# A hybrid backbone's instruction order planned with other costs, its chunk products alternating between row halves, its dense pages moved by 32 bytes

## The chip, the cores and the metric

The kernel runs on one core of one Trainium2 chip. TensorE (PE, with its weight loads PEld), VectorE (DVE), ScalarE (ACT) and GpSimd (POOL) compute; SyncE (SP) issues nearly all DMAs. The metric is the device time of one execution in microseconds, as a median of runs. Lower is better.

## The reference

Two layers over 512 latent tokens and 256 context tokens of width 1024, all in float32. The first mixes by windowed attention and by a bidirectional RWKV-7 scan, the second by a two-dimensional Fourier transform per channel group; each is followed by a squared-ReLU MLP of width 4096. Norms are adaptive (shift, scale and gate come from the conditioning vectors). Cut to what matters:

```
z = h @ w_in ; zc = hc @ w_in                       # one input projection, both streams
att = window_attention(q, k, v, kc, vc, sink)       # softmax over a window, all context keys, a sink
S <- S diag(w) - (S kk)(kk*a)^T + v k^T ; y = S r   # RWKV-7, both directions, context state first
x = x + gt1 * (concat(att, rw) @ w_out)
x = x + gt2 * (square(relu(h2 @ w1)) @ w2)          # channel MLP, both layers
f = fft2(h groups, axes=(tokens, channels)).real @ fourier_w_out   # mixer of the second layer
out = rmsnorm(x, final_g)                           # latent stream only
```

The context stream is not needed after the first layer's mixer, so the kernel computes for it only what the scan's start state and the attention's context keys take.

## The kernel before

**Numbers.** Dense products are made in float32r: each operand is split into a high part (ACT, a cast) and a low part (DVE, a subtraction), and `mm3` issues three matmuls: low x high, high x high, high x low. A weight page is 128x512 (`st` by DMA, then `whi`, `wlo`); a moving page is 128x512 (`hhi`/`hlo` for the normalised stream, `zhi`/`zlo` for the MLP's hidden values). Small products (scan, inverses, attention's value product) are plain float32, which the chip runs as two passes, so each has two records in the profile.

**Stages.** Adaptive norm of layer 0 and the input projection (to about 200 us), the scan, the inverses and attention (to about 560 us), the output projection, MLP 0 (to about 960 us), the Fourier mixer (to about 1060 us), MLP 1.

**The scan.** It runs in chunks of 64 tokens, two directions at once. Six pairs of token blocks (i = 0 to 5; 0 and 1 are context) have two chunks each (j). For a pair, `prep` loads pages (th, kk, r, k) that were spilled to DRAM and makes per chunk and direction the tiles `pr` (key and receptance, scaled by the decay) and `gq`. `chunkmats` multiplies them (`ps<-pr,gq`): for each half `hh` of the partitions (two heads are stacked on 128 partitions) four products `hp`, one tile of PSUM per half, which DVE masks into `ab` and `ed`. `ed` goes to DRAM and comes back later. `inverse` inverts the triangular blocks of `ab` with DVE, small DMAs of 16 KB and 32x32 matmuls. `chain_u`, `chain_s`, `chain_y` are the serial scan over the chunks.

**The order.** `body` doesn't issue anything. It records every operation with the `Plan` class; line 657 then issues all of them, so nearly every instruction has that line in the profile. `Plan.solve` is a list scheduler: it gives every operation a rank (longest way to the end by the costs of `cost`), and simulates the five engines. Whenever an engine is free it takes the ready operation with the highest rank. On the way it models:

- TensorE's granted clock: windows of `WIN` = 3413.3 ns, an activity share above `WARM` switches to full clock, one under `COLD` back to half; `fill` puts `warm` matmuls (line 647) into gaps. A matmul with another tile shape than the last (`r.mode`) costs `MODE` = 100 ns more; among the eight best, one of the same shape is preferred if its key is within `STICK`.
- DMAs: a queue with one server `srv`; a transfer ends 750 ns after its service. SP issues in the order of the plan, and an issue that has to wait holds all behind it.
- Memory: a tile is claimed by the first operation that uses it. If no buffer is free, the operation is parked; when any tile is released, the parked ones are tried again in the order in which they were parked. PSUM's eight banks are shared by four kinds (`mm`, `rk`, `ch`, `iv`), and `BANKS` says how many of them each kind can count on: a claim has to leave those of the other kinds free.

**Memory places.** The pools `const`, `wp`, `H` come first; then `P0`, `P` and `Q` follow each other at one place. `Q`'s pages, tag `zq` (34 of them), hold the hidden values of the MLPs and the Fourier stage's tiles. Tiles start at multiples of 32 bytes. `body` declares a small tile ahead of Q's others, which nothing reads or writes:

```
    Q.tile([128, 8], F32, name="zpad")
```

`solve` keeps only tiles that are used, `self.tiles = {m: t for m, t in self.tiles.items() if t["uses"]}`, so zpad isn't placed before. In the compiled program before, the `zq` pages start at multiples of 64 bytes, the pages of `H` 32 bytes past a multiple of 64.

Of the kernel before, what the change touches and what calls it, by code (L numbers as in the profile page):

```python
# [5 lines left out]
F32 = mybir.dt.float32  # L6
# [197 lines left out]
class Rec:  # L204


    __slots__ = ("eng", "op", "args", "kw", "acc", "lead", "n", "claims", "mode", "load", "piece")
# [31 lines left out]
class Plan:  # L239
# [5 lines left out]
    WIN, COLD, WARM = 3413.3, 0.27, 0.66  # L245
    MODE, STICK = 100, 1500
    KEEP, RAISE, SPARE = 0.7, 0.9, 100
    RING = {"mm": 3, "rk": 2, "ch": 2, "iv": 1}
    BANKS = {"mm": 2, "rk": 1, "ch": 2, "iv": 1}
# [87 lines left out]
    def cost(self, r):  # L337
# [4 lines left out]
        if r.eng == "tensor":  # L342
# [3 lines left out]
            r.mode = up(k), up(m)  # L346
# [4 lines left out]
            f = {(128, 128): 1.0, (64, 128): 0.95, (128, 64): 0.58 if w <= 64 else 0.49 if w <= 128 else 0.27, (64, 64): 0.53, (128, 32): 0.12}.get(r.mode, 0.47)  # L351
# [3 lines left out]
            h = f * (w / 1.2 + 4) if w >= 64 else 110.0 * f if w < 16 else f * (w + 3)  # L355
            r.load *= min(1.0, w / 1.2 / h)
            return 2 * h, h + max(245, w / 1.2 + 175)
        if r.eng == "scalar":
            d = 185 + 0.86 * n
            if r.op == "activation" and any(isinstance(r.kw.get(x), bass.AP) for x in ("scale", "bias")):  # L360
                d += 70
            if abs(ins[0].ap[-1][0]) > 1:
                d += 0.85 * n
            return max(d - 96, 55), d
        if r.eng == "vector":
# [3 lines left out]
            if r.op == "tensor_scalar" and n > 64:  # L369
                d -= 0.3 * n  # L370
            return max(d - 83, 55), d
# [8 lines left out]
        return max(d - 45, 55), d  # L380


    def solve(self):
# [60 lines left out]
        srv, lastmode = 0.0, None  # L444
# [77 lines left out]
        while sched < n:  # L522
# [17 lines left out]
            if e == "tensor" and lastmode:  # L540
                c = []
                while avail[e] and len(c) < 8:
                    c.append(heapq.heappop(avail[e]))
                pick = 0
                for q, (x, kk) in enumerate(c):
                    if recs[kk].mode == lastmode and x < c[0][0] + self.STICK:
                        pick = q
                        break
                k = c.pop(pick)[1]
# [6 lines left out]
            if e == "tensor":  # L556
                if lastmode and r.mode != lastmode:
                    t += self.MODE
                lastmode = r.mode
                c = clock(t)  # L560
                busy(t, hold / c, r.load)
                hold, lat = hold / c, lat - hold + hold / c
            start[k], te[e], end[k] = t, t + hold, t + lat
            if r.op == "dma_start":
# [14 lines left out]
                end[k] = srv + 750  # L579
# [24 lines left out]
            if rel and parked:  # L604
                pq, parked[:] = parked[:], []
# [8 lines left out]
    def issue(self, tc):  # L614
# [12 lines left out]
        def pool_of(name):  # L627
            if name not in pools:
# [4 lines left out]
                place.append(name)  # L633
            return pools[name]
# [31 lines left out]
def body(tc, I, out):  # L666
# [497 lines left out]
    def chunkmats(i, j):  # L1164
# [6 lines left out]
        for d in range(2):  # L1171
# [3 lines left out]
            for hh in range(2):  # L1175
                rows = slice(64 * hh, 64 * hh + 64)
# [933 lines left out]
```

## Time and profile before

| | |
|---|---|
| median of 3 runs | 1420.98 us (1417.09 to 1421.83) |
| profiled execution: time, span | 1418.5 us, 1416.7 us |
| granted TensorE clock, mean | 0.962 |
| PE busy | 1339.2 us (95%), 10752 matmuls |
| PEld busy | 1088.7 us (77%) |
| DVE / ACT / POOL busy | 816.6 (58%) / 642.1 (45%) / 326.7 us (23%) |
| DMA moved | 204.69 MB, 144 GB/s |

Matmuls are pipelined: one of 512 columns lasts some 390 ns in the profile, but the next starts some 230 ns after it. So "busy" says little of how fast PE goes, and rates have to be read as a count in a stretch of time. Granted clock is 1.00 at full speed and 0.50 where the throttle halves it. "SPq" is SP's time to issue, "issue" time in which an engine waited for nothing that the profile shows. An idle engine that is not on the chain costs nothing.

### The profile page before, as it was taken

How to read it: one execution, taken by the hardware profiler on the slowest of the kernel's cores; microseconds unless marked ns; L12 is line 12 of the kernel's file. 1: busy time of each engine (PE TensorE's matmuls, PEld its weight loads, DVE VectorE, ACT ScalarE, POOL GpSimd, SP SyncE). 2: the span in 40 equal slices, each digit the busy share in tenths (PEclk: the TensorE clock that was granted, in tenths of full speed). 3: DMA queues.
4: the chain of work that ended last, by engine and by line, in shares of the span. 5: the costliest groups of instructions: out<-in, count | busy, mean ns of one | idle time of the engine just before them, and what ended most of it. 6: DMA issues, size and time to landing. Idle time of an engine off the chain costs nothing.

```text
span 1416.7 us, 27647 instructions
## 1 busy us (share of the span) xinstructions
PE 1339.2 (95%) x10752; PEld 1088.7 (77%) x10752; DVE 816.6 (58%) x1516; ACT 642.1 (45%) x1289; POOL 326.7 (23%) x359
## 2 busy tenths in 40 slices
PE   6999989979888999999999999999989999999997
PEld 2787877767757777878887888878977888888886
DVE  3844497776876344778655566675976332333334
ACT  3775576365452225446522345333636522255322
POOL 1546485344361413050000000000560000000001
PEclk9999998989987899999999999999999999999999
DMA  9468975565545213226655565662312322223222
GB/s 366 155 193 266 300 243 168 123 174 151 143 117 153 79 34 103 89 76 201 193 171 185 179 190 183 195 199 68 105 61 81 103 91 96 97 91 104 90 89 75
DMA packets 173939, 204.69 MB, mean 144 GB/s; under 512 B 52008, under 2 KB 87912, under 8 KB 173808
## 3 DMA queue, kind: packets, MB, share of 16 engines
q1 hardware_dynamic: 171920, 200.99, 45.5%
q8 instruction: 84, 1.38, 0.4%
q10 hardware_dynamic: 1376, 1.90, 0.4%
q14 instruction: 47, 0.39, 0.1%
q0 software_dynamic: 512, 0.03, 0.0%
HBM read 177.41 MB, written 25.43 MB: 143 GB/s over the span
## 4 chain that ended last, share of the span: by engine, by line
PE 75%; DVE 10%; DMA 5%; issue 3%; ACT 3%; SPq 2%; POOL 1%; DVEq 0%; ACTq 0%; POOLq 0%
PE ps L657 74%; SPq L657 2%; DMA st<-adaA_in 1%; DVE wlo L657 1%; DVE ht L657 1%; DVE gq L657 1%; DMA st<-adaB_in 1%; DMA st<-win_in 1%; DVE Minv L657 1%; DVE wb L657 0%; PE warm L647 0%; DVE ab L657 0%; POOL pgth L657 0%; DVE fwlo L657 0%; DMA st<-fw_in 0%
## 5 line engine op out<-in xcount | busy, mean ns | idle before, releaser
L657 ACT CAST whi<-st 128x512 fp32r<-128x512 f32 x306 | 187.6, 620 | 414.6 <-PE ps L657 376.6
L657 DVE TENSOR_TENSOR wlo<-st,whi 128x512 fp32r<-128x512 f32 x306 | 223.7, 741 | 220.2 <-ACT whi L657 161.7
L657 PE MATMUL ps<-hlo,whi 128*128 128x512 f32 x600 | 230.9, 396 | 2.8 <-DVE hlo L657 2.8
L657 PE MATMUL ps<-hhi,whi 128*128 128x512 f32 x600 | 230.6, 397 | 1.9 <-ACT hhi L657 1.7
L657 PE MATMUL ps<-hhi,wlo 128*128 128x512 f32 x600 | 228.2, 396 | 0.3 <-DVE wlo L657 0.3
L657 PE MATMUL ps<-zhi,whi 128*128 128x512 f32 (+1 forms) x528 | 203.2, 389 | 1.9 <-ACT whi L657 1.9
L657 PE MATMUL ps<-zlo,whi 128*128 128x512 f32 (+1 forms) x528 | 202.2, 389 | 0.0
L657 PE MATMUL ps<-zhi,wlo 128*128 128x512 f32 (+1 forms) x528 | 199.5, 390 | 1.0 <-DVE wlo L657 1.0
L657 PEld LDWEIGHTS ps<-hlo,whi 128*128 128x128 f32 x600 | 113.5, 190 | 27.0 <-DVE hlo L657 4.3
L657 PEld LDWEIGHTS ps<-hhi,whi 128*128 128x128 f32 x600 | 113.2, 189 | 27.2 <-ACT hhi L657 2.6
L657 PEld LDWEIGHTS ps<-hhi,wlo 128*128 128x128 f32 x600 | 113.4, 189 | 23.8 <-DVE wlo L657 0.8
L657 PEld LDWEIGHTS ps<-zhi,whi 128*128 128x128 f32 x528 | 98.8, 188 | 25.5 <-ACT whi L657 3.2
L657 PEld LDWEIGHTS ps<-zhi,wlo 128*128 128x128 f32 x528 | 98.8, 188 | 25.0 <-DVE wlo L657 2.8
L657 PEld LDWEIGHTS ps<-zlo,whi 128*128 128x128 f32 x528 | 98.7, 188 | 22.2
L657 POOL TENSOR_TENSOR rs<-ms,pw 128x4 f32<-128x4 f32 (+1 forms) x7 | 6.2, 886 | 408.1 <-DVE ms L657 408.1
L657 POOL TENSOR_TENSOR wa<-st 128x512 f32<-128x512 f32 x8 | 14.4, 1797 | 342.6 <-DMA st<-fw_in 322.1
L657 POOL TENSOR_TENSOR ada<-ada,sB 128x512 f32<-128x512 f32 x48 | 65.7, 1389 | 33.4 <-DMA ada<-adaB_in 24.9
L657 DVE CUSTOM_DVE_ANT_0 st<-st,sB,vec 128x512 f32<-128x512 f32 x56 | 43.0, 768 | 43.2 <-DMA st<-adaB_in 42.3
L657 DVE TENSOR_TENSOR zlo<-s,zhi 128x512 fp32r<-128x512 f32 x64 | 44.2, 691 | 27.0 <-ACT zhi L657 26.8
L657 PE MATMUL ps<-pr,gq 64*128 64x128 f32 (+1 forms) x384 | 43.5, 328 | 11.2 <-DVE gq L657 11.2
L657 PEld LDWEIGHTS ps<-pr,gq 64*128 64x128 f32 x384 | 39.1, 228 | 17.5 <-issue 9.2
L657 DVE CUSTOM_DVE_ANT_0 st<-st,sB,adv 128x512 f32<-128x512 f32 x56 | 41.9, 749 | 10.0 <-DMA st<-adaB_in 9.4
(401 smaller groups left out, 2557.1 us busy)
## 6 DMA issues: line engine op xcount, KB each, us to landing
st<-w_in SPq DMA_DIRECT2D x256, 256.0 KB, 2.7
st<-adaB_in SPq DMA_DIRECT2D x112, 256.0 KB, 3.2
ada<-adaB_in SPq DMA_DIRECT2D x48, 256.0 KB, 4.6
st<-win_in SPq DMA_DIRECT2D x40, 256.0 KB, 4.4
spl_th<-th SPq DMA_DIRECT2D x16, 384.0 KB, 4.8
pgth<-spl_th SPq DMA_DIRECT2D x24, 256.0 KB, 4.3
st<-adaA_in SPq DMA_DIRECT2D x16, 256.0 KB, 5.1
st<-adaA_in SPq DMA_DIRECT2D x8, 512.0 KB, 7.8
```

What stands on the lines that cost most here:

```text
L657: i = getattr(getattr(tc.nc, r.eng), r.op)(*[tr(a) for a in r.args], **{x: tr(a) for x, a in r.kw.items()})
```

## The change

**The planner's numbers.** `COLD` goes from 0.27 to 0.30 and `WARM` from 0.66 to 0.64. The cost of a float32 matmul is no longer a factor by tile shape: `full` is its time alone (bounded by the weight load), `side` how many run beside each other; `r.place` is the row and column place in the array that it uses (from the partitions of its operands), `taken` how long it holds that place. A matmul waits for its own place; one with another tile shape waits for all places plus `MODE` (`on_array`); among the best eight of one shape, the one whose place is free first is taken. An ACT instruction costs 95 ns for each of scale and bias that is a tensor (70 ns for either or both before); a scan on DVE costs 350 ns more; a DMA ends 1000 ns after its service, not 750; SP can't be more than `DEPTH` = 2400 ns ahead of the DMA server. Parked operations are tried by rank, not by age. `rk` can count on two banks of PSUM instead of one. All these alter the order only.

**chunkmats.** The two PSUM tiles are taken ahead of the products, and the products alternate between the halves: (hp 0, hh 0), (hp 0, hh 1), (hp 1, hh 0) and so on. The masks follow after all eight.

**zpad.** The tile is taken out of `body` and allocated in `issue`, when the pool Q is opened. Q's other tiles start 32 bytes later.

```diff
@@ -204,7 +204,7 @@
 class Rec:
 
 
-    __slots__ = ("eng", "op", "args", "kw", "acc", "lead", "n", "claims", "mode", "load", "piece")
+    __slots__ = ("eng", "op", "args", "kw", "acc", "lead", "n", "claims", "mode", "load", "piece", "place", "taken")
 
 
 class Queue:
@@ -242,11 +242,11 @@
 
     ENGS = ("tensor", "vector", "scalar", "gpsimd", "sync")
     WAIT = {"tensor": 54, "vector": 33, "scalar": 32, "gpsimd": 60, "sync": 60}
-    WIN, COLD, WARM = 3413.3, 0.27, 0.66
-    MODE, STICK = 100, 1500
+    WIN, COLD, WARM = 3413.3, 0.30, 0.64
+    MODE, STICK, DEPTH = 100, 1500, 2400
     KEEP, RAISE, SPARE = 0.7, 0.9, 100
     RING = {"mm": 3, "rk": 2, "ch": 2, "iv": 1}
-    BANKS = {"mm": 2, "rk": 1, "ch": 2, "iv": 1}
+    BANKS = {"mm": 2, "rk": 2, "ch": 2, "iv": 1}
 
     def __init__(self, nc):
         self.nc = nc
@@ -343,22 +343,25 @@
             lhs, rhs = r.args[1], r.args[2]
             k, m, w = lhs.ap[0][1], self.size(lhs), self.size(rhs)
             up = lambda v: 32 if v <= 32 else 64 if v <= 64 else 128
-            r.mode = up(k), up(m)
+            r.mode, r.place, r.taken = (up(k), up(m)), None, 0
             r.load = k * m / 16384
             if rhs.dtype == F32R:
                 r.load *= w / (w + 32.6)
                 return w / 2.4 + 13.6, w / 2.4 + 185
-            f = {(128, 128): 1.0, (64, 128): 0.95, (128, 64): 0.58 if w <= 64 else 0.49 if w <= 128 else 0.27, (64, 64): 0.53, (128, 32): 0.12}.get(r.mode, 0.47)
             if r.op == "transpose":
                 r.load *= 0.49
                 return 109.0, 281.0
-            h = f * (w / 1.2 + 4) if w >= 64 else 110.0 * f if w < 16 else f * (w + 3)
-            r.load *= min(1.0, w / 1.2 / h)
-            return 2 * h, h + max(245, w / 1.2 + 175)
+
+            full = max(w / 1.2 + 4, 111 if m > 64 else 50 if m > 32 else 14 if w < 32 else 27)
+            side = {(64, 128): 1.9, (128, 64): 1.85, (64, 64): 1.8, (128, 32): 4.0, (32, 32): 1.7}.get(r.mode, 1.0)
+            r.place = lhs.offset // lhs.ap[0][0] // r.mode[0], r.args[0].offset // r.args[0].ap[0][0] // r.mode[1]
+            r.taken = 2 * full
+            r.load *= min(1.0, w / 1.2 / full) * side
+            return 2 * full / side, full + max(245, w / 1.2 + 175)
         if r.eng == "scalar":
             d = 185 + 0.86 * n
-            if r.op == "activation" and any(isinstance(r.kw.get(x), bass.AP) for x in ("scale", "bias")):
-                d += 70
+            if r.op == "activation":
+                d += 95 * sum(isinstance(r.kw.get(x), bass.AP) for x in ("scale", "bias"))
             if abs(ins[0].ap[-1][0]) > 1:
                 d += 0.85 * n
             return max(d - 96, 55), d
@@ -368,6 +371,8 @@
                 d += 0.25 * n
             if r.op == "tensor_scalar" and n > 64:
                 d -= 0.3 * n
+            if r.op == "tensor_tensor_scan":
+                d += 350
             return max(d - 83, 55), d
         if r.op == "memset":
             d = 100 + 0.85 * n
@@ -378,6 +383,13 @@
         else:
             d = 250 + 1.2 * n
         return max(d - 45, 55), d
+
+    def on_array(self, t, r, place, last):
+
+        if last and r.mode != last:
+            t = max([t, *place.values()]) + self.MODE
+            place.clear()
+        return max(t, place.get(r.place, 0.0))
 
 
     def solve(self):
@@ -441,7 +453,7 @@
         waiting, avail, te = ({e: [] for e in self.ENGS} for _ in range(2)), None, {e: 0.0 for e in self.ENGS}
         waiting, avail = waiting
         seq, sched = [], 0
-        srv, lastmode = 0.0, None
+        srv, lastmode, place = 0.0, None, {}
         act, clk, clast = {}, {}, [None]
 
         def clock(t):
@@ -538,15 +550,13 @@
                 k = heapq.heappop(waiting[e])[1]
                 heapq.heappush(avail[e], (key[k], k))
             if e == "tensor" and lastmode:
+
                 c = []
                 while avail[e] and len(c) < 8:
                     c.append(heapq.heappop(avail[e]))
-                pick = 0
-                for q, (x, kk) in enumerate(c):
-                    if recs[kk].mode == lastmode and x < c[0][0] + self.STICK:
-                        pick = q
-                        break
-                k = c.pop(pick)[1]
+                pick = [q for q, (x, kk) in enumerate(c) if recs[kk].mode == lastmode and x < c[0][0] + self.STICK]
+                pick.sort(key=lambda q: (max(place.get(recs[c[q][1]].place, 0.0), t), q))
+                k = c.pop(pick[0] if pick else 0)[1]
                 for x in c:
                     heapq.heappush(avail[e], x)
             else:
@@ -554,11 +564,12 @@
             r = recs[k]
             hold, lat = cost[k]
             if e == "tensor":
-                if lastmode and r.mode != lastmode:
-                    t += self.MODE
+                t = self.on_array(t, r, place, lastmode)
                 lastmode = r.mode
                 c = clock(t)
                 busy(t, hold / c, r.load)
+                if r.place:
+                    place[r.place] = t + r.taken / c
                 hold, lat = hold / c, lat - hold + hold / c
             start[k], te[e], end[k] = t, t + hold, t + lat
             if r.op == "dma_start":
@@ -576,7 +587,8 @@
                     row = run if q is a else min(row, run)
                 row = min(row, 4096)
                 srv = max(srv, t + 1400) + nb / row / 16 * (19 + 0.0346 * row)
-                end[k] = srv + 750
+                end[k] = srv + 1000
+                te[e] = max(te[e], srv - self.DEPTH) if e == "sync" else te[e]
             seq.append(k)
             sched += 1
             for q in succS[k]:
@@ -602,7 +614,7 @@
                     else:
                         heapq.heappush(free[g], (relt[m], t_["bank"]))
             if rel and parked:
-                pq, parked[:] = parked[:], []
+                pq, parked[:] = sorted(parked, key=lambda q: key[q]), []
                 for q in pq:
                     enable(q)
         self.span = max(end)
@@ -631,6 +643,8 @@
                 cm = tc.tile_pool(**byname[name].kw)
                 pools[name], ends[name] = cm.__enter__(), cm
                 place.append(name)
+                if name == "Q":
+                    pools[name].tile([128, 8], F32, name="zpad")
             return pools[name]
 
         def tr(a):
@@ -1172,11 +1186,13 @@
             c = j if d == 0 else 1 - j
             if lat:
                 ed = h2("sg", shape=(128, 4, 2, 64), name="ed")
-            for hh in range(2):
-                rows = slice(64 * hh, 64 * hh + 64)
-                p = pst("rk", (128, 4, 128))
-                for hp in range(4):
-                    pe.matmul(p[:, hp, :wd], o.GQ[d][c][rows, hp, :], o.PR[d][c][rows, hp, :wd], start=True, stop=True)
+
+            pp = [pst("rk", (128, 4, 128)) for hh in range(2)]
+            for hp in range(4):
+                for hh in range(2):
+                    rows = slice(64 * hh, 64 * hh + 64)
+                    pe.matmul(pp[hh][:, hp, :wd], o.GQ[d][c][rows, hp, :], o.PR[d][c][rows, hp, :wd], start=True, stop=True)
+            for hh, p in enumerate(pp):
                 mk = K("mAB")[:, 64 * d : 64 * d + 64].unsqueeze(1).to_broadcast([128, 4, 64])
                 dve.tensor_tensor(o.AB[d][:, c, :, hh, :], p[:, :, 0:64], mk, ALU.mult)
                 if lat:
@@ -1796,7 +1812,6 @@
     p2 = ExitStack()
     Q = p2.enter_context(tc.tile_pool(name="Q", bufs=1, reuse_waits="tile"))
     SQP.append(Q)
-    Q.tile([128, 8], F32, name="zpad")
 
     def xt(name):
         return h2("sg", name=name)
```

## The prediction

> **What bounds the kernel now.** I read the busy times by stage first, to see where TensorE (PE) sets the pace and where it doesn't. Columns: stretch in us, busy us of each engine with its instruction count, granted clock, DMA share, GB/s.
>
> ```profile
> core 0: us, PE busy (x) PEld busy (x) DVE busy (x) ACT busy (x) POOL busy (x), PEclk, DMA share, GB/s
> 0.00:50.00 50.00, 34.01 (x159) 18.03 (x159) 24.23 (x47) 25.37 (x52) 17.12 (x27) 0.97 0.86 314
> 50.00:200.00 150.00, 143.66 (x873) 121.47 (x874) 90.99 (x130) 99.68 (x228) 81.64 (x72) 0.99 0.77 240
> 200.00:380.00 180.00, 158.29 (x2722) 129.77 (x2721) 133.20 (x290) 100.48 (x236) 86.55 (x121) 0.87 0.55 149
> 380.00:560.00 180.00, 165.82 (x3067) 129.66 (x3066) 93.45 (x236) 62.89 (x136) 61.31 (x73) 0.87 0.37 103
> 560.00:640.00 80.00, 77.59 (x384) 62.80 (x383) 61.66 (x104) 36.25 (x75) 21.90 (x18) 1.00 0.26 84
> 640.00:797.00 157.00, 156.61 (x677) 126.65 (x676) 94.78 (x197) 61.17 (x106) 0.00 (x0) 1.00 0.59 190
> 797.00:960.00 163.00, 161.13 (x700) 131.05 (x700) 106.76 (x209) 73.16 (x125) 3.13 (x2) 1.00 0.61 192
> 960.00:1060.00 100.00, 95.23 (x621) 85.61 (x620) 73.50 (x105) 43.95 (x96) 42.73 (x34) 0.98 0.23 72
> 1060.00:1417.00 357.00, 346.86 (x1563) 283.69 (x1561) 137.99 (x204) 139.19 (x243) 12.30 (x14) 1.00 0.28 91
> ```
>
> Two kinds of stage. In 640 to 960 and 1060 to 1417 (the two MLPs) PE is busy nearly all the time at full clock: each nanosecond per matmul counts. In 200 to 560 (the scans, inverses and attention) PE is granted 0.87 of its clock. That share says how much ran at half clock: 2 x 0.13 x 360 = 94 us. A busy PE is not the limit there, so the chain of waits was read next, over 200 to 380, then 380 to 560, then 640 to 1060 (the profile cuts these lines where they end here).
>
> ```profile
> by line: PE ps L657 56.9%; SPq L657 7.6%; issue 5.9%; DVE gq L657 4.2%; DMA pgk<-spl_k 2.7%; POOL pgth L657 2.7%; DVE L L657 2.2%; POOL pr L657 1.7%; POOL ada L657 1.6%; ACT pgth L657 1.4%; DMA qd<-qr 1.4%; DVE pgth L657 1.1%; DVE Minv L657
> by line: PE ps L657 55.3%; issue 8.1%; SPq L657 5.8%; DVE Minv L657 4.1%; DMA edd<-ed 2.7%; DVE gq L657 2.0%; DVE mx L657 1.6%; DVE q L657 1.6%; DVE ed L657 1.5%; DVE pp L657 1.5%; DVE scr L657 1.2%; DMA Minv<-Dg 1.2%; DVE y L657 1.2%; DVE
> by line: PE ps L657 82.2%; DMA st<-adaB_in 2.8%; issue 2.1%; DVE wb L657 1.5%; DVE fwlo L657 1.4%; DMA st<-fw_in 1.4%; DVE wlo L657 1.4%; DVE x L657 0.8%; POOL wa L657 0.8%; ACT uhi L657 0.8%; DVE ht L657 0.7%; DVE ab L657 0.7%; ACT fwhi L6
> ```
>
> In 200 to 560 PE holds about 56% of the path; the rest is spread over the SP queue's own issuing, instruction issue, DVE and round trips through DRAM. So a microsecond of PE work saved there is worth some 0.56 us.
>
> **The page offset.** The MLPs stream two kinds of moving tiles: hhi/hlo (pages of the pool H) against w1, zhi/zlo (tag zq of the pool Q) against w2. Here are PE alone in a w2 stretch and a w1 stretch of the second MLP (count in brackets), and the durations of both kinds (min/median/max ns).
>
> ```profile
> 1145.00:1225.00 80.00, 80.00 (x345) 1.00 0.28 92
> 1232.00:1312.00 80.00, 80.00 (x355) 1.00 0.31 99
> L657 PE MATMUL ps<-zhi,whi x528: 277/395/502, 699.5 to 1403.9; 128*128 128x512 f32 x166, 128*128 128x256 f32 x10
> L657 PE MATMUL ps<-hhi,whi x600: 387/389/794, 69.5 to 1315.2; 128*128 128x512 f32 x150
> L657 PE MATMUL ps<-zhi,whi 128*128 128x512 f32 x496 | 195.3, 396 | 1.9 <-ACT whi L657 1.9
> ```
>
> Without a gap in either stretch, a matmul on z costs (80 + 0.4)/345 = 233.0 ns and one on h (80 + 0.4)/355 = 226.5 ns, where 0.4 is the tail of the one already running. The medians differ by the same 6 ns. Weights, width, clock and the PSUM tag are alike; ACT and DVE are less busy in the slow stretch. What differs is the page: in the compiled program before, zhi/zlo start at multiples of 64 bytes (213312 = 3333 x 64), hhi/hlo 32 bytes past one (100448 = 1569 x 64 + 32). The cause is that zpad, 32 bytes at the head of Q, is never used, so the planner drops it (only tiles with uses are placed). The change allocates it when Q is really opened; the pool's other small tiles (ms, rs, wbs) still come ahead of zq, since the first z hangs on the first wbs. So every zq page moves to byte 32, where h is. There are 496 of each of three kinds, 1488 matmuls: 1488 x 6.5 ns = 9.7 us, all on PE's path (0.6% of idle in these stages). Bounds: 0 if the offset isn't the cause, 9.7 if it is; I take 9.7, since the two rates are steady and nothing else in the rows separates them. The Fourier stage's zq tiles are few (192 narrow matmuls) and count as nothing; their cover is the POOL and DVE work that holds that stage.
>
> The Trainium skill speaks against it: SBUF — State Buffer, § Door 1 (the note on "cachelines") gives lines of 16 bytes, so a 2048-byte page that begins at byte 0 or at byte 32 touches equally many, and the offset would gain nothing; the sum below would then be 9.7 us higher. The trace does not agree that pages are alike, at 233.0 against 226.5 ns, but no run so far has moved one page.
>
> **Chunk products on alternating row halves.** chunkmats multiplies PR and GQ on partitions 0-63 (hh 0), four products, then on 64-127 (hh 1). After, the halves alternate, into two PSUM tiles claimed together. Nothing is added: 384 matmul records before and after. Four of their bursts, and all of them by shape:
>
> ```profile
> L657 PE MATMUL ps<-pr,gq x384: 267/272/578, 193.7 to 424.8; 64*128 64x128 f32 x128, 64*128 64x64 f32 x64
> 259.23 1.49 PE L657 MATMUL ps<-pr,gq 64*128 64x128 f32 x16
> 327.75 1.83 PE L657 MATMUL ps<-pr,gq 64*128 64x128 f32 x24
> 197.87 5.76 PE L657 MATMUL ps<-pr,gq 64*128 64x64 f32 x48 [2.16 <-DVE gq L657]
> 418.32 6.74 PE L657 MATMUL ps<-pr,gq 64*128 64x128 f32 x48 [1.82 <-DVE gq L657]
> 198.00:203.00 5.00, 5.00 (x47) 0.65 0.52 161
> 418.40:424.40 6.00, 6.00 (x45) 0.50 0.31 62
> ```
>
> Less the last one's own duration, steps are (1.49 - 0.27)/15 = 81 ns and (1.83 - 0.27)/23 = 68 ns, and in the bursts at low clock (0.65, 0.50) (5.76 - 0.4)/47 = 114 and (6.74 - 0.5)/47 = 133 ns. Weighted by their counts that is 109 ns, 384 x 109 = 42 us in all. The steps of 68 and 81 ns are far under the 272 ns one lasts, and under the 114: where the planner happened to mix halves, they already overlap in part. Bounds: nothing, if the mixing is as good as it gets; half of 42 = 21, if alternation pairs all. I take the best row, 68 ns, for all: 42 - 26 = 16 us of PE work, times 0.56 on the path = 9 us. The masking on DVE now starts after eight products rather than four; the wait for the first half grows by about four steps, 0.3 us, 24 times, under other DVE work (133 of 180 us busy). If that cover failed, it would cost 7.
>
> The Trainium skill has a rule against this too: TensorE: Matmul & The Clock Gate, Part 1, says that the gate grants full clock for activity within a window of 3.4 us and half without. Estimated from that page: 16 us less work is 4.7 windows; were each to fall to half, PE would lose 1.7 us of work in each, 8 us, and the term would be about 1. The 0.87 above agrees that the gate acts in this stage.
>
> **The order planned anew.** Everything else changes numbers that the planner reckons with: matmul times by array place (taken, place; a switch of tile shape waits for all places), scale and bias operands of ACT at 95 ns each, 350 ns more for a scan, 250 ns more for a DMA to land, SP not further ahead of the DMA service than 2.4 us, other activity bounds (COLD, WARM), waiting claims by priority instead of age, two PSUM banks kept for rk instead of one. No instruction but the fill-in warm matmuls is added or removed. What moves can't be read from the diff; what it can be worth is bounded by what the order leaves on the path. In the scan stage SP's own issuing is 0.076 x 180 + 0.058 x 180 = 24 us; below nothing, a single bad move can cost as much as SP's longest wait on PE there:
>
> ```profile
> SPq L657 <- PE ps L657: 92.0, 28, 24.0
> SPq L657 <- DVE ed L657: 40.9, 10, 16.9
> ```
>
> All loads, spills and the 16 KB shuffles of the inverses share SP's one queue in program order, so behind each such wait stand the pages of the next prep and the next ed, and behind those DVE and POOL. I take a quarter of 24, 6 us of gain: better nearness of the plan to the measured steps, and no reason for more. In 640 to 1060 the chain shows adaB and fw loads: (0.028 + 0.014) x 420 = 18 us, loads that came too late. Claims by priority and a truer DMA time act on just that; I take a sixth, 3 us, with ends of 18 gained and one such wait more, 4.1, lost:
>
> ```profile
> DVE st L657 <- DMA st<-adaB_in: 51.8, 45, 4.1
> ```
>
> The bank kept for rk leaves mm three banks instead of four when nothing else is held. In the MLPs a bank is filled for 24 x 226.5 ns = 5.4 us and emptied in one ACT instruction, so three suffice: no cost.
>
> **Sum.** 9.7 + 9 + 6 + 3 = 27.7 us off the profiled execution, whose span is 1416.7 and time 1418.5: 1390.8. That execution is 2.5 us under the median of the runs shown (1421.0), so I predict 1393 for a median.
>
> **Rivals.**
> The page offset does nothing. For it: h and z pages also lie in different regions of the memory, and no row moves one alone. Against: the steadiness of the two rates. Time: 1393 + 9.7 = 1403.
>
> The order gains more. For it: 24 us of SP on the path, 18 us of late loads, 94 us at half clock, all things that a truer plan addresses. Against: the planner had a model of all of them before. With half of what is left of the bounds, (24 - 6 + 18 - 3 + 21 - 9)/2 = 22: 1371.
>
> Slower: one place, SP's queue in the scan stage. The new depth rule and the priority of claims reorder loads against the waits on PE and ed. If a wait of the size of the two longest (24.0 + 16.9 = 41 us) lands ahead of pages that a prep needs, prep, products, inverse and scan step follow one another without other work to fill, and the stage grows by it: 1393 + 41 = 1434. It decides the sign from 28 us on. Against: 360 us hold 92 us of such waits today with 24 us of SP on the path, so most are slack.
>
> No change: the same shift by about 28 us, the plan giving back just what page and products win: 1421.
>
> **How the numbers follow.** Forecast 0.45 (its own range 1380 to 1402), offset without effect 0.13, larger gain 0.22, no change 0.10, slower 0.10. A change under 0.3% (4 us) can't be told from none here. Faster: 0.45 + 0.13 + 0.22 and a third of the no-change case, 0.83; same 0.08; slower 0.09. The range reaches down to the larger gain, 1368, and up to the edge of no change, 1417.
>
> **What would show it.** Offset: the median of zhi falls from 395 to 389 ns and 80 us of w2 hold 355 matmuls. Products: bursts of pr,gq at 68 ns a step or less at full clock. Plan: the stretch that ends at 560 now ends 15 us earlier, SPq's share of its chain falls, adaB leaves the chain. Wrong would be: z still at 233 ns, a scan stage longer than now, or a clock there under 0.87.

## The result and the profile after

The changed kernel takes 1404.5 us (median of 4 runs, 1401.1 to 1408.2) against 1420.5 us beside it: ratio 0.9889, 95% interval 0.9862 to 0.9916, so 12 to 20 us less. Forecast were 1393, with a range of 1368 to 1417. Later, with six runs of the changed kernel and sixteen of the one before on one chip, the ratio was 0.9875 (0.9851 to 0.9899), 1402.8 against 1421.8 us.

First the dense stage. Durations of the matmuls on z and on h (min/median/max, first and last start), then PE alone in 80 us of w2 and 70 us of w1 of MLP 1, all of the changed kernel:

```profile
L671 PE MATMUL ps<-zhi,whi x528: 277/389/499, 694.4 to 1386.5; 128*128 128x512 f32 x165, 128*128 128x256 f32 x11
L671 PE MATMUL ps<-hhi,whi x600: 387/389/795, 68.6 to 1299.9; 128*128 128x512 f32 x150
...
1133.00:1213.00 80.00, 80.00 (x355) 1.00 0.29 96
1222.00:1292.00 70.00, 70.00 (x311) 1.00 0.31 97
```

The median on z fell from 395 to 389 ns, and 80 us hold 355 matmuls where they held 345: (80 + 0.4)/355 = 226.5 ns each, as on h. Next the scan stage by stretches (as the table before the change, with the second stretch ending at 555), the chunk products, the first matmuls of the output projection (rwhi), and the chain from 640 to 1060:

```profile
200.00:380.00 180.00, 159.00 (x2760) 128.55 (x2760) 129.85 (x273) 98.17 (x236) 95.59 (x120) 0.86 0.58 164
380.00:555.00 175.00, 159.14 (x3001) 121.80 (x3001) 88.73 (x226) 62.70 (x136) 60.16 (x73) 0.88 0.38 104
...
L671 PE MATMUL ps<-pr,gq 64*128 64x128 f32 (+1 forms) x384 | 34.2, 291 | 8.1 <-DVE gq L671 5.9 <-DVE ab L671 2.2
...
L671 PE MATMUL ps<-rwhi,whi x32: 389/389/389, 579.4 to 602.5; 128*128 128x512 f32 x32
...
by line: PE ps L671 89.4%; issue 1.9%; DVE wlo L671 1.1%; DMA st<-w_in 1.1%; DVE fwlo L671 0.8%; DVE ht L671 0.8%; DVE x L671 0.8%; DVE ulo L671 0.6%; PE warm L661 0.6%; ACT uhi L671 0.5%; DVE wb L671 0.5%; ACT whi L671 0.4%; DVE hlo L671 0
```

The granted clock there is what it was (0.86 and 0.88 after 0.87), PE is as busy as before, and the products take 34.2 us of busy time. The adaB and fw loads, 2.8% and 1.4% of the chain before, are no longer among its shares. How little the share of one execution says is shown under a_oldrules.

So the profiled executions compare by stage as follows, with the start of rwhi as the border. Before, rwhi starts here:

```profile
L657 PE MATMUL ps<-rwhi,whi x32: 389/389/389, 584.5 to 607.6; 128*128 128x512 f32 x32
```

To that border 584.5 against 579.4: 5 us less. From it to the end of the span 1416.7 - 584.5 = 832.2 against 1399.3 - 579.4 = 819.9: 12 us less. These are single executions; others of the same two orders are set beside them further down.

### The profile page after: what moved, and what is told of

It reads as the page before. It is cut to its first block, busy times and chain, and to the rows that moved or that the text cites. A ratio compares the mean times of both kernels' runs of the same rounds, so it can differ in the third digit from the quotient of the medians.

```text
span 1399.3 us, 27577 instructions
## 1 busy us (share of the span) xinstructions
PE 1321.8 (94%) x10746; PEld 1078.7 (77%) x10746; DVE 812.9 (58%) x1516; ACT 642.5 (46%) x1289; POOL 324.8 (23%) x359
## 4 chain that ended last, share of the span: by engine, by line
PE 79%; DVE 7%; DMA 6%; issue 3%; ACT 2%; SPq 2%; POOL 1%; DVEq 0%; ACTq 0%; POOLq 0%
PE ps L671 79%; SPq L671 2%; DMA st<-adaA_in 1%; DMA Minv<-Dg 1%; DVE Minv L671 1%; DVE gq L671 1%; DVE wlo L671 1%; DMA c<-cT_in 1%; DVE ht L671 1%; DMA vu<-vtd 1%; PE warm L661 1%; ACT gq L671 0%; DMA ada<-adaB_in 0%; DMA qb<-qd 0%; DMA x<-xT_in 0%
## 5 line engine op out<-in xcount | busy, mean ns | idle before, releaser
L671 PE MATMUL ps<-hhi,wlo 128*128 128x512 f32 x600 | 230.8, 399 | 1.3 <-DVE wlo L671 1.3
L671 PE MATMUL ps<-zhi,whi 128*128 128x512 f32 (+1 forms) x528 | 200.1, 384 | 1.5 <-ACT whi L671 1.5
L671 PE MATMUL ps<-zhi,wlo 128*128 128x512 f32 (+1 forms) x528 | 195.8, 383 | 0.0
L671 POOL TENSOR_TENSOR pT<-pT 128x512 f32<-128x512 f32 x28 | 36.9, 1332 | 28.8 <-ACT pT L671 28.6
L671 PEld LDWEIGHTS ps<-pr,gq 64*128 64x128 f32 x384 | 30.1, 195 | 15.5 <-issue 7.1
```

The source lines that it names most:

```text
L671: i = getattr(getattr(tc.nc, r.eng), r.op)(*[tr(a) for a in r.args], **{x: tr(a) for x, a in r.kw.items()})
```

## The experiments

All kernels below compute all that the reference asks for, with the instructions of the kernel that they start from. Only a_oldrules and a_mode101 have another order, with a few `warm` matmuls more or less, and a_pitch, which has one page less.

### The page alone: b_page32 and a_page0

b_page32 gives the kernel before the 32 bytes; a_page0 takes them from the changed kernel. The planner knows nothing of this tile, so the order stays.

```diff
# a_page0, from the changed kernel
-                if name == "Q":
-                    pools[name].tile([128, 8], F32, name="zpad")
# b_page32, from the kernel before
+                if name == "Q":
+                    pools[name].tile([128, 8], F32, name="zpad")
```

> The kernel before with the 32-byte tile alone, its old order unchanged. Theory (offset): 9.7 us less than the kernel before, ratio 0.993, zhi at 389 ns. Rival (offset gives nothing by itself, or the stage waits for loads instead): ratio 1.000. If theory holds, the order and the products together are worth 16 - 9.7 = 6 us.

> The changed kernel without the 32-byte tile, so that the zq pages are at byte 0 again; the order of all instructions is that of the changed kernel. Theory (offset): 1488 matmuls at 233.0 instead of 226.5 ns, 9.7 us longer than the changed kernel beside it, about 1414, and the median duration of zhi back at 395 ns. Rival (the new order made z faster, not the page): the same time as the changed kernel, zhi at 389 ns.

Beside them the changed kernel was measured again.

> The changed kernel itself, to have it beside the others on one chip. Expected as in its first four runs, 1401 to 1408 us, with two groups of times (near 1401 and near 1408): if the groups come from where the clock windows fall in the scan stage, the runs with the lower mean clock are the longer ones.

Measured: a_again 1402.8 us (ratio 0.9875, 0.9851 to 0.9899); a_page0 1412.0 (0.994, 0.9918 to 0.9962); b_page32 1412.7 (0.9935, 0.9914 to 0.9956). Added to the old order the page gives 1421.8 - 1412.7 = 9.1 us, taken from the new one it costs 1412.0 - 1402.8 = 9.2 us. The two add up: what the page doesn't explain, the order and the products, is 1421.8 - 1412.0 = 9.8 us. The page's part is known to some 3 us on the old order and some 5 us on the new one, by these intervals. As to the two groups that a_again expected: the first four runs of the changed kernel look like it (1401.1 and 1401.4 us at mean clocks of 0.963 and 0.967, 1407.6 and 1408.2 us at 0.957 and 0.960), but the six of a_again don't. They spread from 1398.8 to 1406.3 us, and 1402.7 and 1406.3 us have the same clock, 0.962.

The rows of b_page32 and then of a_page0, for z, and PE alone in 80 us of w2 of each:

```profile
L659 PE MATMUL ps<-zhi,whi x528: 277/389/501, 700.5 to 1395.2; 128*128 128x512 f32 x166, 128*128 128x256 f32 x10
1140.00:1220.00 80.00, 80.00 (x355) 1.00 0.30 96
```

```profile
L669 PE MATMUL ps<-zhi,whi x528: 276/395/498, 696.1 to 1396.4; 128*128 128x512 f32 x165, 128*128 128x256 f32 x11
1138.00:1218.00 80.00, 80.00 (x345) 1.00 0.28 92
```

389 ns and 355 matmuls with the page at byte 32, 395 ns and 345 with the page at byte 0, whatever the order. The place of the page is the cause, and it is worth what the prediction reckoned.

### Which offset, and relative to what: a_curve, a_pitch, a_page64, a_weights0, a_all0

a_curve gives the z pages 528 columns and starts the data at another column in each of the four stretches.

```diff
-                hi, lo = zq("zhi"), zq("zlo")
+                g = 4 * (2 * l + half)
+                hi, lo = (zq(n + "abcd"[2 * l + half], shape=(128, 528))[:, g : g + 512] for n in ("zhi", "zlo"))
```

> The changed kernel with pages of 528 columns for zhi and zlo, of which 512 are used from column 0, 4, 8 and 12 in the four stretches (MLP 0 first and second half, MLP 1 first and second half): the moving data start at bytes 32, 48, 0 and 16 past a multiple of 64. Order as in the changed kernel. Theory (only where the data start within 64 bytes counts): 226.5 ns a matmul at byte 32 and 233 at byte 0, with bytes 16 and 48 either between (229 and 229) or with one of the two. Rival (16-byte lines alone): all four alike, at 226.5. Rival (the page's place in the memory as a whole): all four alike, since all four stretches use the same pages.

None of the three came: 1407.4 us (one run), and no stretch ran at the good rate. The medians of zhi's durations from the first stretch to the last:

```profile
L671 PE MATMUL ps<-zhia,whi x128: 388/392/402, 694.6 to 788.9; 128*128 128x512 f32 x128
L671 PE MATMUL ps<-zhib,whi x128: 387/393/504, 871.2 to 964.4; 128*128 128x512 f32 x128
L671 PE MATMUL ps<-zhic,whi x128: 388/396/400, 1120.7 to 1217.8; 128*128 128x512 f32 x128
L671 PE MATMUL ps<-zhid,whi x144: 275/392/452, 1297.4 to 1392.8; 128*128 128x512 f32 x112, 128*128 128x256 f32 x32
```

Byte 32 itself (zhia) has 392, not 389. Start to start, over 300 to 370 matmuls of each stretch, that is 230.8, 232.5, 232.9 and 231.7 ns. The pages being 2112 bytes apart changed something that the offset doesn't say. a_pitch takes pages 2176 bytes apart, so that all of a stretch start alike within 128 bytes:

```diff
-        return Q.tile(list(shape), dt, tag="zq", bufs=34, name=name)
+        return Q.tile(list(shape), dt, tag="zq", bufs=33, name=name)
-                hi, lo = zq("zhi"), zq("zlo")
+                g = (0, 4, 8, 16)[2 * l + half]
+                hi, lo = (zq(n + "abcd"[2 * l + half], shape=(128, 544))[:, g : g + 512] for n in ("zhi", "zlo"))
```

> The changed kernel with pages of 544 columns (2176 bytes, a multiple of 128) for zhi and zlo and 33 of them instead of 34, of which 512 columns are used from column 0, 4, 8 and 16 in the four stretches: bytes 96, 112, 0 and 32 past a multiple of 128; all pages of a stretch agree in that. In the run before this, pages of 2112 bytes gave 230.8 ns even at byte 32 past a multiple of 64, so the offset within 64 bytes alone isn't all. Theory (the offset within 128 bytes, alike from page to page, decides): 226.9 ns in the first stretch, about 233 in at least one other. Rival (only pages a multiple of 2048 bytes apart can run at 226.9): some 231 in all four.

The theory fell (1410.3 us, one run). The durations on the first of the two z pages, from the first stretch to the last:

```profile
L671 PE MATMUL ps<-zhia,whi x128: 387/391/397, 698.5 to 792.2; 128*128 128x512 f32 x128
...
L671 PE MATMUL ps<-zhib,whi x128: 388/395/502, 875.1 to 967.1; 128*128 128x512 f32 x128
...
L671 PE MATMUL ps<-zhic,whi x128: 390/396/400, 1123.8 to 1220.7; 128*128 128x512 f32 x128
...
L671 PE MATMUL ps<-zhid,whi x144: 275/391/450, 1300.3 to 1395.7; 128*128 128x512 f32 x112, 128*128 128x256 f32 x32
```

Start to start, both pages together, these are 229.8, 229.4, 232.6 and 231.6 ns. With pages this far apart no offset runs steadily at 226.5; what the distance between pages does stays open. The next kernels keep pages 2048 bytes apart and move whole pools.

```diff
# a_page64
-                    pools[name].tile([128, 8], F32, name="zpad")
+                    pools[name].tile([128, 16], F32, name="zpad")
# a_weights0, where issue opens the first pools
+            if p.name in ("wp", "H"):
+                pools[p.name].tile([128, 8], F32, name="pad")
# a_all0, at the same place
+            if p.name == "wp":
+                pools[p.name].tile([128, 8], F32, name="pad")
```

> The changed kernel with a 64-byte tile at the head of Q, so that zq pages are 2048 bytes apart and start at byte 0 of 128 (the kernel before: byte 64, the changed kernel: byte 96). Same order. Theory (the half of the 64 bytes in which the page starts decides): 233 ns on z, 1412 us. Rival (byte 64 of 128 was bad by itself): 226.9 ns, 1403 us.

> The changed kernel with 32-byte tiles at the head of the weight pool and of H: the weight pages whi and wlo start at byte 0 past a multiple of 64 instead of 32; hhi, hlo, zhi and zlo stay at byte 32. Same order. Theory (the moving page alone decides): h and z at 226.9 ns, 1403 us. Rival (moving and stationary page have to start alike): both at 233 ns, some 1500 + 1800 matmuls at 6.4 ns more, 20 us longer, about 1423 us.

> The changed kernel with a 32-byte tile at the head of the weight pool: the weight pages, H's pages and Q's pages all start 32 bytes later, at byte 0 past a multiple of 128, moving and stationary alike. Same order. In the runs so far 226.9 ns stood where the moving page was at byte 96 of 128 and the weights too; 233.3 where the moving page was at 64, 0 or 32 of 128, each time with the weights in the other half of the 64 bytes. Theory (moving and stationary page have to start alike within 64 bytes): 226.9 ns on h and z, the changed kernel's 1403 us. Rival (the moving page has to start at byte 32 of 64, wherever the weights are): 233.3 ns on both, some 3300 matmuls at 6.4 ns more, 21 us longer, 1424 us.

a_page64 took 1415.9 us, a_weights0 1426.1 (one run each, beside 1424.2 for the kernel before), a_all0 1405.0 (ratio 0.989, 0.9861 to 0.9918). PE alone, in w2 of a_page64; then in w2 and w1 of a_weights0; then in w2 and w1 of a_all0:

```profile
1140.00:1220.00 80.00, 80.00 (x344) 1.00 0.29 97
```

```profile
1150.00:1230.00 80.00, 80.00 (x344) 1.00 0.29 93
1245.00:1310.00 65.00, 65.00 (x280) 1.00 0.30 93
```

```profile
1134.00:1214.00 80.00, 80.00 (x355) 1.00 0.30 96
1225.00:1290.00 65.00, 65.00 (x288) 1.00 0.31 97
```

The starts of the pages in the compiled programs, in bytes past a multiple of 128, beside the rates from these rows (stretch + 0.4, divided by the count):

| kernel | weights | h | ns on h | z | ns on z |
|---|---|---|---|---|---|
| before | 96 | 96 | 226.5 | 64 | 233.0 |
| changed | 96 | 96 | 226.4 | 96 | 226.5 |
| a_page0 | 96 | 96 | | 64 | 233.0 |
| a_page64 | 96 | 96 | | 0 | 233.7 |
| a_weights0 | 0 | 32 | 233.6 | 32 | 233.7 |
| a_all0 | 0 | 0 | 227.1 | 0 | 226.5 |

"Byte 32" was not the point. a_weights0 has both moving pages at byte 32 of 64 and is slow on both, a_all0 has them at byte 0 and is fast. What fits all six kernels is the distance between the weight page and the moving page. In the fast rows it is a multiple of 128 bytes, in the slow ones an odd multiple of 32 (modulo 2048 it is 0 or 256 bytes against 32, 224 or 288). Distances of 64 and of 128 bytes, modulo 256, were not among them. So whether it is enough that both start in the same half of 64 bytes, as a_all0 had it, isn't shown, and neither is the reason. In a_weights0 I had meant h and z to stay at byte 96 of 128; the two small tiles moved them to 32, so that run changed two things, and a_all0 was needed to tell them apart.

### The chunk products: a_oldproducts, b_newproducts

The record order of chunkmats is put back in the changed kernel, and put alone into the kernel before.

```diff
# a_oldproducts, from the changed kernel (b_newproducts: the same, the other way, from the kernel before)
-            pp = [pst("rk", (128, 4, 128)) for hh in range(2)]
-            for hp in range(4):
-                for hh in range(2):
-                    rows = slice(64 * hh, 64 * hh + 64)
-                    pe.matmul(pp[hh][:, hp, :wd], ...)
-            for hh, p in enumerate(pp):
+            for hh in range(2):
+                rows = slice(64 * hh, 64 * hh + 64)
+                p = pst("rk", (128, 4, 128))
+                for hp in range(4):
+                    pe.matmul(p[:, hp, :wd], ...)
```

> The changed kernel with the chunk products in their old record order (all of one half, then the other) and all of the new planner. Theory (products and plan each gave some of the 10 us that the page doesn't explain, the products most of it, as the prediction's 9 against 6): 5 to 9 us longer than the changed kernel, 1408 to 1412. Rival (the new planner's own choice by array place pairs the halves anyway): the same time, bursts of pr,gq no slower than 60 to 80 ns a step.

> The kernel before with the chunk products recorded in turns on the row halves, its planner and pages unchanged. Theory (PE work saved at 0.56 on the path): the bursts of pr,gq at 60 ns a step in place of 81 and more, 4 to 9 us less, ratio 0.994 to 0.997. Rival (the old planner, which reckons nothing for the pairing and keeps one bank for rk, loses elsewhere what it wins): ratio 1.000 within 0.002.

a_oldproducts took 1405.1 us (0.9895, 0.9864 to 0.9927), 2 us more than the changed kernel and within its interval; b_newproducts 1423.4 us (1.0014, 0.9989 to 1.0038), no gain. The reason is in the compiled programs. That of a_oldproducts is the changed kernel's, byte for byte on all five engines, and that of b_newproducts is the kernel before's. So these two are repeats, and their 2 us show how far two measurements of one program differ. Matching each record with the compiled program tells which half a product reads. Where two products directly follow each other, the next one is on the other half in:

| kernel | other half | same half |
|---|---|---|
| before | 58 | 112 |
| b_newproducts | 58 | 112 |
| a_oldproducts | 128 | 44 |
| changed | 128 | 44 |
| a_oldrules (below) | 94 | 76 |

The record order decides nothing, in either planner: the list scheduler takes products by key, and the old one's choice never looks at the halves. The alternation comes from the new planner; that it is its choice by place is argued from the code, and a_oldrules, which keeps that choice, has less of it. Two bursts of the changed kernel at full clock, one in turns on the halves and one on a single half, then the products' busy time in a_oldproducts and in b_newproducts (34.2 us in the changed kernel, above):

```profile
235.41 1.16 PE L671 MATMUL ps<-pr,gq 64*128 64x128 f32 x16 [1.17 <-DVE gq L671]
...
256.89 1.16 PE L671 MATMUL ps<-pr,gq 64*128 64x128 f32 x8
```

```profile
L671 PE MATMUL ps<-pr,gq 64*128 64x128 f32 (+1 forms) x384 | 38.2, 313 | 9.9 <-DVE gq L671 6.9 <-DVE R L671 1.6 <-DVE ab L671 1.4
```

```profile
L657 PE MATMUL ps<-pr,gq 64*128 64x128 f32 (+1 forms) x384 | 45.3, 332 | 9.2 <-DVE gq L657 8.8 <-DVE Xs L657 0.4
```

(1.16 - 0.27)/15 = 59 ns a step in turns, under the 68 that were forecast; on a single half, eight records take as long as these sixteen. But the whole of the products, summed from each record to the next matmul, went only from 46.8 us to 38.5 (39.8 in a_again, 41.7 in a_oldproducts). Waits don't explain that: single gaps of more than 0.4 us inside the bursts add up to 5.2 us before and 6.2 after. Without them, two records of a burst start 82 ns apart on average at full clock before and 74 ns after, with 44 of the 172 neighbours still on one half. At half clock it is 147 and 130 ns, and fewer records are there: 113 of the 384 before, 23 in the changed kernel (80 in a_oldproducts). About half of what the steps lost is this change of clock, not the pairing.

### The planner's rules: a_oldrules, a_mode101

a_oldrules puts back three rules: the bank for rk, the claims by age, the DMA's end and depth. a_mode101 makes a change without meaning.

```diff
# a_oldrules
-    BANKS = {"mm": 2, "rk": 2, "ch": 2, "iv": 1}
+    BANKS = {"mm": 2, "rk": 1, "ch": 2, "iv": 1}
-                end[k] = srv + 1000
-                te[e] = max(te[e], srv - self.DEPTH) if e == "sync" else te[e]
+                end[k] = srv + 750
-                pq, parked[:] = sorted(parked, key=lambda q: key[q]), []
+                pq, parked[:] = parked[:], []
# a_mode101
-    MODE, STICK, DEPTH = 100, 1500, 2400
+    MODE, STICK, DEPTH = 101, 1500, 2400
```

> The changed kernel with three rules of the old planner: one bank kept for rk, parked claims by age, a DMA ends 750 ns after its service and SP isn't held back; the new matmul and ACT costs, places and activity bounds stay. Theory (claims by rank and the truer DMA give 3 us in the MLPs and some in the scan stage): 3 to 6 us longer than the changed kernel, adaB back on the chain between 640 and 1060. Rival (the order as such is worth nothing, any plan falls within a few us): within 3 us of the changed kernel, either way.

> The changed kernel, the planner's price for a change of tile shape set to 101 ns in place of 100: a change that means nothing, but gives another order. It tells how far the time scatters from plan to plan. Theory (the plan's gain is real and stable): within 2 us of the changed kernel. Rival (one plan differs from the next by as much as the order's gain): 4 us or more away, in either direction.

a_mode101 took 1402.5 us (0.9883, 0.9847 to 0.9919), the changed kernel's time. Its compiled order does differ, in 120 of the 1228 places of DVE's sequence and 45 of the 914 of SP's; so the gain isn't one lucky order, as far as one other order tells. a_oldrules took 1415.6 us (0.9969, 0.9944 to 0.9995). That is 13 us more than the changed kernel, over twice what was expected, and no better than the kernel before with the page alone (1412.7). So the new costs and places without the new rules are worth nothing that can be told here, and the 9.8 us need the rules. Whether the rules alone would bring them, under the old costs, was not tried. Where they act, by its output projection and its chain from 640 to 1060:

```profile
L670 PE MATMUL ps<-rwhi,whi x32: 388/389/390, 590.1 to 613.3; 128*128 128x512 f32 x32
...
by line: PE ps L670 89.7%; issue 1.9%; DVE wlo L670 1.2%; DVE sq L670 1.0%; DVE x L670 1.0%; DMA st<-adaB_in 0.8%; DVE ulo L670 0.7%; DVE ht L670 0.7%; DVE fwlo L670 0.6%; PE warm L660 0.5%; ACT uhi L670 0.5%; DVE st L670 0.4%; DVE xn L670 
```

rwhi starts at 590.1, 11 us after the changed kernel's. From there to the end it takes 1410.9 - 590.1 = 820.8 us against 819.9. So nearly all of the loss lies ahead of the output projection, and the 3 us that the expectation put in the MLPs are not there. adaB is on the chain with 0.8%, as expected, but that says little. Here is the same stretch of a_page0, which has the order of the changed kernel, and of b_newproducts, which is the program of the kernel before:

```profile
by line: PE ps L669 87.3%; issue 2.3%; DMA st<-adaB_in 2.1%; DVE wlo L669 1.3%; DMA st<-w_in 1.0%; DVE ht L669 0.8%; DVE x L669 0.8%; DVE fwlo L669 0.7%; DVE ulo L669 0.6%; PE warm L659 0.6%; DVE wb L669 0.5%; DVE hlo L669 0.4%; ACT whi L66
```

```profile
by line: PE ps L657 88.9%; DVE wb L657 1.5%; DVE fwlo L657 1.4%; DMA st<-fw_in 1.4%; issue 1.3%; POOL wa L657 0.9%; DVE x L657 0.8%; DVE ab L657 0.7%; ACT fwhi L657 0.5%; ACT uhi L657 0.5%; DVE ht L657 0.5%; DVE wlo L657 0.3%; ACT ax L657 0
```

adaB has 2.1% with the new order, and none with the old one, where the kernel before had 2.8%: its share differs more between executions of one order than between the orders. Which of the three rules carries the gain was not tried.

## Why the prediction was right or wrong

The sign, the worth of the page and the range held. The size was forecast at 27.7 us and came out at 16 to 19, and 1404.5 us lies outside the forecast's own 1380 to 1402. The total alone would have misled: it is next to the 1403 of the rival in which the page does nothing, while in fact the page gave all of its 9 us and the order and the products fell short. That the wide range held is no proof of the terms.

**The page offset: right.** 1488 x 6.5 ns = 9.7 us were reckoned; 9.1 and 9.2 us measured, in two orders. The rival that it does nothing fell, and with it the reading of the Trainium skill's page SBUF — State Buffer, § Door 1 (lines of 16 bytes, so byte 0 and byte 32 alike): the runs show 233.0 and 226.5 ns. The reason given was half right, and here luck helped. I compared h and z and took byte 32 for the good place; a_weights0 and a_all0 show that what counts is the place against the weights', which h happened to share.

**The chunk products: wrong.** The term was 9 us, and the step that failed is the first, that the edit in chunkmats makes the products alternate. It changes the records, and the planner orders them; with and without it the compiled programs are the same, in both planners, so this part of the change is worth nothing. The alternation that came is the new planner's. The second step, the 16 us of PE work, failed as well. The 109 ns are an average over two bursts at full clock (68 and 81 ns) and two at low clock (114 and 133), and the 68 ns put in their place come from full clock. So much of the difference was clock and not pairing. Added up without the waits, the steps were 36.5 us before and 28.0 after (31.7 in a_oldproducts), where 42 and 26 were reckoned. The third step, 0.56 us for each us of PE work, no run tests. The share itself is unsteady: PE holds 56.9% of the chain from 200 to 380 us in the kernel before and 47.9% in b_newproducts, the same program.

**The order in the scan stage: the size wrong together with the products.** 9 and 6 us were forecast to the output projection; 5 came in the two profiled executions. Others of the same orders scatter as much as that. With the old order rwhi starts at 584.5, 593.3 (b_newproducts) and 585.6 us (b_page32), on average at 587.8. With the new one it starts at 579.4, 578.4 (a_again), 584.0 (a_oldproducts), 581.1 (a_page0), 585.2 (a_page64) and 580.8 (a_all0), on average at 581.5. So some 6 us is the better figure. SPq's share of the chain from 200 to 380 us, which was to fall, is 7.1% after 7.6%, and 1.2% in b_newproducts, so it tells nothing. What the new order did do is start the products earlier, and that head start got lost. In each of the two fences below, the first row is the chunk products', the second the loads of the adaptive weights (ada), the third those of vu, the scan's first operand, the fourth the scan's first products. The first fence is of the kernel before, the second of the changed one:

```profile
L657 PE MATMUL ps<-pr,gq x384: 267/272/578, 193.7 to 424.8; 64*128 64x128 f32 x128, 64*128 64x64 f32 x64
L657 SPq DMA_DIRECT2D ada<-adaB_in x48: 328/406/1197, 57.9 to 212.6; - x48
L657 SPq DMA_DIRECT2D vu<-vtd x24: 450/500/864, 220.5 to 514.8; - x24
L657 PE MATMUL ps<-vu,ab x352: 219/222/368, 277.6 to 529.3; 128*64 128x64 f32 x176
```

```profile
L671 PE MATMUL ps<-pr,gq x384: 272/272/579, 157.2 to 427.5; 64*128 64x128 f32 x128, 64*128 64x64 f32 x64
L671 SPq DMA_DIRECT2D ada<-adaB_in x48: 327/424/1487, 60.6 to 273.9; - x48
L671 SPq DMA_DIRECT2D vu<-vtd x24: 450/520/1349, 274.4 to 510.8; - x24
L671 PE MATMUL ps<-vu,ab x352: 219/222/370, 278.2 to 528.0; 128*64 128x64 f32 x176
```

The products start 36 us earlier (157.2 after 193.7). The price is the ada loads, which now end at 273.9 instead of 212.6. ada and vu share the five pages of the tag cp, and a tag's tiles are claimed in the order of the records, so vu can't be loaded before the last ada: at 274.4 instead of 220.5. The scan starts when it did, 278.2 after 277.6 (283.1 and 282.8 in b_newproducts and b_page32). PE waits 1.1 us for the landing of this vu before the scan's first product, and DMA vu<-vtd has 4.5% of the chain from 200 to 380 us, where the kernel before has none. The chain of the changed kernel from 268 us on shows work on ada and its last loads, and right behind them the clearing of the second pair of vu's:

```profile
271.15 1.28 POOL ada L671
...
273.42 2.94 DMA ada<-adaB_in
...
276.49 3.30 POOL ada L671 x2
...
279.84 0.70 POOL vu L671
```

So a new wait took up the head start. That giving vu pages of its own would free it is argued from these rows, and was not tried. From 278 to the output projection the stretch went from 306.9 to 301.2 us in these two executions.

**The dense stages' order: the size about right, the reason not borne out.** 3 us forecast; between the start of rwhi and the end, a_page0 needs 1409.3 - 581.1 = 828.2 us. The old order needs 832.2 in the kernel before and 1422.2 - 593.3 = 828.9 in b_newproducts, all with the old page. With the new page the old order needs 1408.0 - 585.6 = 822.4 (b_page32) and the new one 819.9 and 1397.0 - 578.4 = 818.6 (a_again). That makes 1 to 4 us. The reason given was that claims by priority and a truer DMA time keep adaB and fw off the chain. But a_oldrules has neither and needs no longer (820.8), and adaB comes and goes from one execution to the next. Which part of the new order gives these few us stays open. The borders in a_page0 and in b_newproducts:

```profile
L669 PE MATMUL ps<-rwhi,whi x32: 389/389/389, 581.1 to 604.2; 128*128 128x512 f32 x32
```

```profile
L657 PE MATMUL ps<-rwhi,whi x32: 388/389/390, 593.3 to 616.4; 128*128 128x512 f32 x32
```

**The rivals.** Slower by SP's queue: no sign of it, the stage got shorter; but a_oldrules, 11 us later at the output projection, shows that a plan of this kind can give back all that the others win there. The larger gain (1371) and no change (1421) lie outside what was measured. The loss of clock reckoned from the Trainium skill's page TensorE: Matmul & The Clock Gate, Part 1, which would have cost the products' gain, isn't borne out by the clock of the stage, 0.87 before and 0.86 and 0.88 after.

## What to carry to other kernels

Where two streams of the same matmul run at steadily different rates, compare the start addresses of their moving and stationary pages before looking at loads and engines: a 32-byte tile moved 1488 matmuls by 6.5 ns each. In a kernel whose order is planned, an edit to the order of the records may do nothing; compare the compiled programs first. Before you average steps of matmuls, sort them by granted clock. Before you read a share of the chain, read it in a second execution of the same program. And before pricing an earlier start, ask what else shares the buffers of the step that comes after it.

## What the runs showed of the hardware

A float32r matmul of 512 columns takes 226.4 to 227.1 ns start to start when the moving and the stationary page lie a multiple of 128 bytes apart, and 233.0 to 233.7 when they lie an odd multiple of 32 apart, in six kernels with pages 2048 bytes apart; other distances were not run. With pages 2112 and 2176 bytes apart all offsets tried gave between 229.4 and 232.9 ns, the alike ones too; why is open. At full clock, 16 records of chunk products that alternate between the row halves take 1.16 us, 59 ns apart on average, and 8 records on a single half take as long. Two measurements of one program on one chip (a_again and a_oldproducts) differ by 2 us of 1400 in their medians, and by 6 us in where the output projection starts in the profiled execution.
